# A hybrid decoder layer on one core: kept output weights in buffers of their own, the first value products in a written order, one more dense chunk ahead of GLA's first levels

## Chip, cores, metric

The kernel runs on one core of a Trainium2 chip. The metric is the device time of one execution in microseconds (us); a kernel's time is the median of its runs. The engines are called by the names of the profile: PE is TensorE (PEld its weight loads), DVE is VectorE, ACT is ScalarE, POOL is GpSimd and SP is SyncE, which issues nearly all DMAs. A program keeps instructions of one engine in order; an engine that waits holds up all that stands behind on it.

## What is computed

One layer over 512 tokens of 1024 channels, all in float32. RMSNorm; one input projection `w_in` of 7696 columns, which feeds three branches and their gates: gated linear attention (GLA, 4 heads, chunked, with a low-rank decay), block-sparse softmax attention (MoBA, 8 heads) and a short gated convolution. Each branch is projected to 1024 channels and weighted by a sigmoid gate; the sum goes through an output projection, a norm and a residual add. Then a channel mixer: norm, up-projection to 2 x 2816, a depthwise convolution of width 3, a SiLU gate, the down-projection, a norm and a residual add.

```python
h = rmsnorm(x, g_mix_pre[l])
(gq, gk, gv, gr, glr, mq, mk, mv, sb, sc, sx, glog) = split_cols(h @ w_in[l], IN_SPLITS)
br_a = gla_mixer(gq, gk, gv, gr, glr, gla_w_lr2[l], gla_b_lr[l], gla_norm[l])
br_b = moba_mixer(mq, mk, mv)
br_c = sb * causal_dwconv(sc * sx, sc_conv_w[l])
merged = (gates[..., 0, :] * (br_a @ w_br_gla[l]) + gates[..., 1, :] * (br_b @ w_br_moba[l])
          + gates[..., 2, :] * (br_c @ w_br_sc[l])).astype(x.dtype)
x = x + rmsnorm(merged @ w_out[l], g_mix_post[l])
h = rmsnorm(x, g_ffn_pre[l])
u = causal_dwconv(h @ ffn_w_up[l], ffn_conv_w[l]) + ffn_conv_b[l]
y = (jax.nn.silu(u[..., :D_FF]) * u[..., D_FF:]) @ ffn_w_down[l]
x = x + rmsnorm(y, g_ffn_post[l])
```

## The kernel before

**Products in three parts.** Each float32 operand is split into a high part (`whi`, `hh`, ...: a copy by ScalarE to a shorter format) and a low part (`wlo`, `hl`: VectorE subtracts the high part from the operand). `mm3` (L93) issues three matmuls for each product: high x high, high x low, low x high. A weight tile of 128x1024 is loaded into `raw` (2 buffers), split by `split_w` (L84 and L85) into `whi` and `wlo` (5 buffers each), and then read by 24 matmuls or more. The 128x512 accumulators are PSUM tiles, 3 with the tag "main" and 5 with the tag "side".

**Who sets the order.** PE's order is that of the program text (a manual schedule over the whole layer). The order of ScalarE, VectorE and GpSimd is chosen by a scheduler when the kernel is built, but for the start block (`with tc.manual_schedule(...)` for both), where it is the text's as well.

**Start.** PE runs 14 matmuls on zeros (`warm`, L203), then two matmuls with a row of ones (L207) that spread the gain `grow` over 128 partitions; VectorE copies the two results into `g1` (L208). For each of 4 token tiles of 128: ScalarE squares x and sums (L161), VectorE and GpSimd make the reciprocal root of the mean (L138, L140), VectorE multiplies x by it and by g1 into h (L163), PE transposes h in 8 matmuls (L171), ScalarE and VectorE split the result into `hh` and `hl` (L175, L176). Then the value products: 24 matmuls with 272 columns (256 value columns and the 16 low-rank columns, unit u = 0) and 24 with the other 256 (u = 1). In each half of 4 contraction tiles the three parts alternate. VectorE copies the sums to `v` and `lrt` (L254, L256). The weights of both units come by `load_v` as two pieces of 512 KB each on SP's queue, the 16 columns on ScalarE's queue (L187), and are split at L239 and L244. The transposes of the next tile stand between the two units. The value products end where the transposes of the convolution weights (L326) begin.

**Dense columns and GLA.** The rest of `w_in` is a stream of chunks of 12 matmuls of 128x512 (`cols_cm`, `mm3c`). `main.beside(gen)` interleaves it with a side generator: for each number n that the generator yields, n chunks of the stream go to PE. For each of two channel tiles `ct`, `gla_pair` issues the products across chunks (L486), copies them to `ac` (L489), yields 1, and goes on to the first group of levels: `decayed` makes the operands E (VectorE L509 and L515, ScalarE L510 and L511, GpSimd L514), PE multiplies them (L529 to L532) into PSUM tiles that must be free of the products across.

**Output projection and first up-projection products.** `row_major` keeps 8 accumulators (4 token tiles x 2 halves of 512 columns) and adds contraction tiles 0 to 3 to all of them. Tiles 4 to 7 (`resident` = 4) are split too and kept, and are then added for one token tile after the other, so that each tile's epilogue runs beside the next one's products. `first_up`, called in between, loads and splits the four weight tiles of the first up-projection unit in the same 5 buffers. The epilogue `epi1` squares the sums (L784), makes the statistic (L791, L793), writes x (L796), squares and normalises x into h (L161, L163), and at the last tile issues the first 256 columns of the up-projection (`up_mm`) with the transposes of tiles 2 and 3 between them.

Of the kernel before, what the change touches and what calls it, by code (L numbers as in the profile page):

```python
# [8 lines left out]
F32 = mybir.dt.float32  # L9
# [6 lines left out]
P = 128  # L16
# [15 lines left out]
def hybrid_layer(ctx: ExitStack, tc: tile.TileContext, x, g_mix_pre, w_in, gla_w_lr2, gla_b_lr,  # L32
# [45 lines left out]
    def split_w(src, a, b, sub=None, urgent=True):  # L78
        with tc.high_priority() if urgent else nullcontext():
            hi = wp.tile([P, 1088], F32R, tag="whi", name=nm("whi"), bufs=5)  # L80
            lo = wp.tile([P, 1088], F32R, tag="wlo", name=nm("wlo"), bufs=5)
            hv = hi[:, :a * b].rearrange("p (a b) -> p a b", a=a)
            lv = lo[:, :a * b].rearrange("p (a b) -> p a b", a=a)
            nc.scalar.activation(hv, src, AF.Copy)  # L84
            (sub or nc.vector).tensor_tensor(lv, src, hv.bitcast(F32), op=OP.subtract)  # L85
        return hv, lv

# [67 lines left out]

    st = pool("start", bufs=2, side="right")

    def normed(xt, g, pl):
        ss = sp.tile([P, 1], F32, tag="ss", name=nm("ss"))
        h = pl.tile([P, D], F32, tag="h", name=nm("h"))  # L160
        nc.scalar.activation(h, xt, AF.Square, accum_out=ss)  # L161
        r = rstd(ss, 1, 1.0 / D)
        nc.vector.scalar_tensor_tensor(h, xt, r, g, op0=OP.mult, op1=OP.mult)  # L163
        return h

    def transposed_split(h, th, tl, t, ps_):
        for b in range(2):
# [7 lines left out]
            nc.scalar.activation(hv, pv, AF.Copy)  # L175
            nc.vector.tensor_tensor(lv, pv, hv.bitcast(F32), OP.subtract)  # L176

    def load_v(u):
        raw = rw.tile([P, 2176], F32, tag="raw", name=nm("vraw"))
        n = 272 if u == 0 else 256  # L180
        rv = raw[:, :8 * n].rearrange("p (k c) -> p k c", k=KD)
        c = C_GV + 256 * u
        for k in (0, 4):
            nc.sync.dma_start(rv[:, k:k + 4, :256],
                              w_in[k * P:(k + 4) * P, c:c + 256].rearrange("(k p) c -> p k c", p=P))
            if u == 0 and k == 0:
                nc.scalar.dma_start(rv[:, :, 256:], w_in[:, C_LR:C_LR + 16].rearrange("(k p) c -> p k c", p=P))  # L187
            yield
        yield rv
# [11 lines left out]
    ps = psum()  # L201
    for _ in range(14):
        nc.tensor.matmul(ps, warm[:, :P], warm, start=True, stop=True)  # L203

    for n in range(2):
        ps = psum()
        nc.tensor.matmul(ps, ones, grow[:, n * 512:(n + 1) * 512], start=True, stop=True)  # L207
        nc.vector.tensor_copy(g1[:, n * 512:(n + 1) * 512], ps)  # L208
# [5 lines left out]
    vraw = [list(load_v(0))[-1]]  # L214
    load_x(1)
    vraw.append(list(load_v(1))[-1])
# [18 lines left out]
    def hi_v(u, half):  # L235
        n = 272 if u == 0 else 256
# [9 lines left out]
    def v_mm(ps, t, u, half):  # L246
        n = 272 if u == 0 else 256
        ts_ = slice(t * P, (t + 1) * P)
        hi, lo = wv[u, half]
        mm3(ps[:, :n], [(hh[:, 4 * half + k, ts_], hl[:, 4 * half + k, ts_], hi[:, k], lo[:, k]) for k in range(4)],  # L250
            start=half == 0, stop=half == 1)
# [223 lines left out]
    def gla_pair(ct, across):  # L475
# [14 lines left out]
        yield 1  # L490
# [246 lines left out]
    h2l = h2p.tile([P, KD, T], F32R, name="h2l")  # L737
    ep = pool("epi", bufs=3, side="right")
# [7 lines left out]
    def row_major(w, kk, resident, getl, epilogue, middle=None):  # L746
# [170 lines left out]
```

## Time and profile before

| what | us |
|---|---|
| median of 3 runs | 898.33 (896.80 to 899.42) |
| the profiled execution | 898.33 |
| its span, from the first to the last instruction | 896.5 |
| busy in the span: PE / DVE / ACT / POOL | 880.6 / 454.1 / 337.6 / 75.0 |

A profile line of a timeline gives the start, the time taken, the engine, the line of the kernel, the operation, what it writes and reads, and how often it stands there in a row (x8); behind it, in brackets, how long the engine had been idle and what ended that. A line of the waits gives an engine and line, what it waited for, the total, the number of times and the longest. A window is a stretch of the span with the busy time of an engine in it and the TensorE clock that was granted, 1.00 being full.

### The profile page before, as it was taken

To read this page: it belongs to the slowest core of one execution; us is meant where nothing else is said; L and a number is where in the kernel's file an instruction comes from. 1 tells how busy PE (TensorE), PEld (TensorE's weight loads), DVE (VectorE), ACT (ScalarE), POOL (GpSimd) and SP (SyncE) were. 2 spreads that over 40 slices of the span, in tenths; PEclk is the share of its full clock that TensorE was granted. 3 is DMA by queue.
4 is the path that set the end of the run, shared out by engine and by line. 5 is a ranking of instruction groups with operands and counts; after the bars stand their busy time and mean duration, and the time that the engine had idled before them with its cause. 6 is when DMAs were issued, how large, how long until landed. Compare 5 with 4: busy or idle time off the path is not lost.

```text
span 896.5 us, 11496 instructions
## 1 busy us (share of the span) xinstructions
PE 880.6 (98%) x4723; PEld 728.7 (81%) x4723; DVE 454.1 (51%) x715; ACT 337.6 (38%) x511; POOL 75.0 (8%) x87
## 2 busy tenths in 40 slices
PE   8999999999999999999999989999999999999997
PEld 5988788987777888888888889888888888888885
DVE  5723766487763242423424486655555555533324
ACT  5236654244543223232322355433333333322222
POOL 1000421131100020101101010000000000000000
PEclk8999999999999999999999999999999999999999
DMA  8241231131211324133265123223333322222202
GB/s 264 69 145 51 91 93 51 48 95 49 93 48 48 117 71 131 58 117 94 72 229 169 48 94 95 94 95 98 104 105 107 103 96 94 94 94 94 94 0 94
DMA packets 68616, 85.33 MB, mean 95 GB/s; under 512 B 2693, under 2 KB 62291, under 8 KB 68564
## 3 DMA queue, kind: packets, MB, share of 16 engines
q1 hardware_dynamic: 67522, 84.53, 29.7%
q8 instruction: 37, 0.61, 0.3%
q10 hardware_dynamic: 1042, 0.07, 0.1%
q14 instruction: 15, 0.12, 0.0%
HBM read 82.50 MB, written 2.10 MB: 94 GB/s over the span
## 4 chain that ended last, share of the span: by engine, by line
PE 93%; ACT 3%; DVE 2%; DMA 1%; issue 1%; POOL 0%; ACTq 0%; DVEq 0%; POOLq 0%
PE ps L93 86%; PE ps L633 1%; PE ps L675 1%; PE ps L565 1%; PE ps L658 1%; DMA vraw<-in_w_in_dram 1%; PE ps L531 1%; DMA raw<-in_ffn_w_up_dram 1%; PE ps L171 1%; ACT whi L84 0%; DVE wlo L85 0%; DVE h L163 0%; ACT L432 0%; ACT whi L239 0%; ACT E L510 0%
## 5 line engine op out<-in xcount | busy, mean ns | idle before, releaser
L85 DVE TENSOR_TENSOR wlo<-raw,whi 128x1024 fp32r<-128x1024 f32 x142 | 178.3, 1257 | 235.2 <-ACT whi L84 235.1
L84 ACT ACTIVATE whi<-raw 128x1024 fp32r<-128x1024 f32 x142 | 149.8, 1057 | 253.8 <-PE ps L93 241.1
L93 PE MATMUL ps<-hh,whi 128*128 128x512 f32 x416 | 165.8, 398 | 0.0
L93 PE MATMUL ps<-hh,wlo 128*128 128x512 f32 x416 | 162.2, 390 | 0.0
L93 PE MATMUL ps<-hl,whi 128*128 128x512 f32 x416 | 162.1, 390 | 0.0
L93 PE MATMUL ps<-h2h,whi 128*128 128x512 f32 (+1 forms) x384 | 143.4, 374 | 0.0
L93 PE MATMUL ps<-h2h,wlo 128*128 128x512 f32 (+1 forms) x384 | 143.3, 373 | 0.0
L93 PE MATMUL ps<-h2l,whi 128*128 128x512 f32 (+1 forms) x384 | 143.2, 373 | 0.0
L93 PEld LDWEIGHTS ps<-hh,whi 128*128 128x128 f32 x416 | 78.1, 188 | 19.4 <-issue 3.2
L93 PEld LDWEIGHTS ps<-hh,wlo 128*128 128x128 f32 x416 | 78.1, 188 | 16.8
L93 PEld LDWEIGHTS ps<-hl,whi 128*128 128x128 f32 x416 | 78.2, 188 | 15.3
L93 PEld LDWEIGHTS ps<-h2h,wlo 128*128 128x128 f32 x384 | 73.0, 190 | 12.6
L93 PEld LDWEIGHTS ps<-h2l,whi 128*128 128x128 f32 x384 | 73.0, 190 | 12.5
L93 PEld LDWEIGHTS ps<-h2h,whi 128*128 128x128 f32 x384 | 73.1, 190 | 12.4
L93 PE MATMUL ps<-whi,ahi 128*128 128x512 f32 x176 | 68.5, 389 | 0.0
L93 PE MATMUL ps<-wlo,ahi 128*128 128x512 f32 x176 | 68.5, 389 | 0.0
L93 PE MATMUL ps<-whi,alo 128*128 128x512 f32 x176 | 68.5, 389 | 0.0
L879 DVE TENSOR_TENSOR alo<-a,ahi 128x512 fp32r<-128x512 f32 x22 | 15.2, 692 | 55.9 <-ACT ahi L878 55.9
L878 ACT ACTIVATE ahi<-a 128x512 fp32r<-128x512 f32 x22 | 13.9, 632 | 75.4 <-PE ps L93 65.4
L724 POOL TENSOR_TENSOR gate<-gate 128x512 f32<-128x512 f32 x16 | 24.0, 1502 | 216.7 <-DVE gate L722 200.1
L93 PE MATMUL ps<-whi,hh 128*128 128x256 f32 (+1 forms) x128 | 38.4, 300 | 0.9 <-ACT hh L175 0.9
L93 PEld LDWEIGHTS ps<-wlo,ahi 128*128 128x128 f32 x176 | 33.0, 188 | 6.9
(196 smaller groups left out, 1181.5 us busy)
## 6 DMA issues: line engine op xcount, KB each, us to landing
raw<-in_w_in_dram SPq DMA_DIRECT2D x28, 1024.0 KB, 5.5
raw<-in_ffn_w_up_dram SPq DMA_DIRECT2D x22, 1024.0 KB, 5.1
raw<-in_ffn_w_down_dram SPq DMA_DIRECT2D x11, 1024.0 KB, 4.9
x<-in_x_dram SPq DMA_DIRECT2D x8, 512.0 KB, 7.2
raw<-in_w_out_dram SPq DMA_DIRECT2D x4, 1024.0 KB
vraw<-in_w_in_dram SPq DMA_DIRECT2D x4, 512.0 KB, 6.5
raw<-in_w_br_gla_dram SPq DMA_DIRECT2D x4, 512.0 KB, 3.6
raw<-in_w_br_moba_dram SPq DMA_DIRECT2D x4, 512.0 KB, 3.4
```

Of the source, the lines that this page charges most:

```text
L84: nc.scalar.activation(hv, src, AF.Copy)
L85: (sub or nc.vector).tensor_tensor(lv, src, hv.bitcast(F32), op=OP.subtract)
L93: last = nc.tensor.matmul(ps, l, r, start=start and i == 0 and j == 0, stop=stop and i == n - 1 and j == 2)
L171: nc.tensor.transpose(ps[:, i * P:(i + 1) * P], h[:, k * P:(k + 1) * P], ident)
L531: nc.tensor.matmul(pv[0:64, t], kl[hs, lo], qr[hs, lo], start=True, stop=True)
L565: nc.tensor.matmul(po[:, c], l, v[:, j, cv], start=j == 0, stop=j == i)
L633: nc.tensor.matmul(out_[i, e][:, :n], mq[hs, pair, i * P:(i + 1) * P], mk[hs, pair, :n], start=True, stop=True)
L658: nc.tensor.transpose(ps[:, (i - j) * P:(i - j + 1) * P], pr[i][:, j * P:(j + 1) * P], ident)
L675: nc.tensor.matmul(po[64 * e:64 * e + 64, j * P:], mv[:, j, hd * 64:(hd + 1) * 64], pts[e][j], start=j == 0, stop=j == NT - 1)
L724: nc.gpsimd.tensor_tensor(g, g, acc, op=OP.add)
L878: nc.scalar.activation(hi, a[:, k], AF.Copy)
L879: nc.vector.tensor_tensor(lo, a[:, k], hi.bitcast(F32), OP.subtract)
```

## The change

Three places change; the sums computed are the same.

1. **Start.** 8 warm-up matmuls, the two gain broadcasts, 7 warm-ups, the transposes, 1 warm-up. ScalarE copies the gain to `g1` in halves, VectorE's first multiply is in halves. The 16 low-rank columns move from the first unit to the second, and with them their DMA on ScalarE's queue; the first unit is now the upper 256 value columns. `v_mm` issues all 8 high x high, then 8 low x high, then 8 high x low products; the next tile's transposes come before the last 8 of the second unit. ScalarE copies the sums to `v`. The first split of the dense column weights is pinned behind the last copy to `hh`.
2. **GLA.** `yield 2 - ct`: for ct = 0, two chunks of the stream instead of one stand between the products across and the first levels; the stream's last stretch, behind MoBA, has 96 matmuls instead of 108.
3. **Output projection.** `keep_out` gives the kept tiles 4 and 5 homes in `ahi`/`alo` (four halves of 128x512, buffers that the down-projection uses later) and tiles 6 and 7 in a new pool `khi`/`klo`. The five whi/wlo buffers are then free for the up-projection's splits.

```diff
-    def split_w(src, a, b, sub=None, urgent=True):
...
+    def split_w(src, a, b, home=None):
+        with tc.high_priority():
+            if home is None:
+                home = [wp.tile([P, 1088], F32R, tag=tag, name=nm(tag), bufs=5) for tag in ("whi", "wlo")]
+            hv, lv = [z[:, :a * b].rearrange("p (a b) -> p a b", a=a) for z in home]
+            ins = nc.scalar.activation(hv, src, AF.Copy)
+            if first_splits:
+                after(ins, first_splits.pop(), "the start's own copies come first")
+            nc.vector.tensor_tensor(lv, src, hv.bitcast(F32), op=OP.subtract)
         return hv, lv
...
     def load_v(u):
-        n = 272 if u == 0 else 256
+        n = 272 if u else 256
-        c = C_GV + 256 * u
+        c = C_GV + 256 * (1 - u)
+        if u:
+            nc.scalar.dma_start(rv[:, :, 256:], w_in[:, C_LR:C_LR + 16].rearrange("(k p) c -> p k c", p=P))
...
-    for _ in range(14):
-        nc.tensor.matmul(ps, warm[:, :P], warm, start=True, stop=True)
...
+    warm_up(8)
+    gps = [psum() for _ in range(2)]
     for n in range(2):
-        nc.tensor.matmul(ps, ones, grow[:, n * 512:(n + 1) * 512], start=True, stop=True)
-        nc.vector.tensor_copy(g1[:, n * 512:(n + 1) * 512], ps)
+        nc.tensor.matmul(gps[n], ones, grow[:, n * 512:(n + 1) * 512], start=True, stop=True)
+    warm_up(7)
...
+    def v_mm(ps, t, u, before_lo=None):
+        for j, (l, part) in enumerate(((hh, 0), (hl, 0), (hh, 1))):
+            if j == 2 and before_lo:
+                before_lo()
+            for k in range(KD):
+                nc.tensor.matmul(ps[:, :n], l[:, k, ts_], wv[u, k // 4][part][:, k % 4],
+                                 start=j == 0 and k == 0, stop=j == 2 and k == KD - 1)
...
     def v_out(ps, t, u):
-        nc.vector.tensor_copy(v[:, t, u * 256:(u + 1) * 256], ps[:, :256])
-        if u == 0:
+        nc.scalar.activation(v[:, t, (1 - u) * 256:(2 - u) * 256], ps[:, :256], AF.Copy)
+        if u:
             nc.vector.tensor_copy(lrt[:, t, :16], ps[:, 256:272])
...
     with tc.manual_schedule(engines={nc.scalar.engine, nc.vector.engine}):
-        hn = normed(xts[0], g1, st)
+        ss, hn = squares(xt, st)
+        halves = [slice(n * 512, (n + 1) * 512) for n in range(2)]
+        for n in range(2):
+            nc.scalar.activation(g1[:, halves[n]], gps[n], AF.Copy)
         hi_v(0, 0)
-        lo_v(0, 0)
+        r = rstd(ss, 1, 1.0 / D)
+        for n in range(2):
+            nc.vector.scalar_tensor_tensor(hn[:, halves[n]], xt[:, halves[n]], r, g1[:, halves[n]],
+                                           op0=OP.mult, op1=OP.mult)
+        transposed_split(hn, hh, hl, 0, psum, (lambda: lo_v(0, 0), None))
+        warm_up(1)
         hi_v(0, 1)
-        transposed_split(hn, hh, hl, 0, psum)
         lo_v(0, 1)
         for t in range(NT):
             pa, pb = psum("main"), psum("main")
+            v_mm(pa, t, 0)
             if t < 3:
                 hn = normed(xts[t + 1], g1, st)
             if t == 0:
                 for half in range(2):
                     hi_v(1, half)
                     lo_v(1, half)
-            for half in range(2):
-                v_mm(pa, t, 0, half)
-            if t < 3:
-                transposed_split(hn, hh, hl, t + 1, psum)
             v_out(pa, t, 0)
-            for half in range(2):
-                v_mm(pb, t, 1, half)
+            v_mm(pb, t, 1, (lambda: transposed_split(hn, hh, hl, t + 1, psum)) if t < 3 else None)
             v_out(pb, t, 1)
+            if t == 2:
+                first_splits.append(last_hi[0])
...
-        yield 1
+        yield 2 - ct
...
+    kp = pool("kept", bufs=2, side="right")
...
-                wts.append([z[:, 0] for z in split_w(raw[:, e:e + 1], 1, D)])
+                if keep and kt >= kk - resident:
+                    wts.append(keep(kt, raw[:, e:e + 1]))
+                else:
+                    hl_ = split_w(raw[:, e:e + 1], 1, D)
+                    wts.append([[z[:, 0, n * 512:(n + 1) * 512] for n in range(2)] for z in hl_])
...
+    def keep_out(kt, src):
+        if kt >= 6:
+            home = [kp.tile([P, D], F32R, tag=tag, name=nm(tag)) for tag in ("khi", "klo")]
+            return [[z[:, 0, n * 512:(n + 1) * 512] for n in range(2)] for z in split_w(src, 1, D, home)]
+        halves = []
+        for n in range(2):
+            home = [ah.tile([P, T], F32R, tag=tag, name=nm(tag)) for tag in ("ahi", "alo")]
+            halves.append([z[:, 0] for z in split_w(src[:, :, n * 512:(n + 1) * 512], 1, 512, home)])
+        return [[halves[n][z] for n in range(2)] for z in range(2)]
...
-    row_major(w_out, KD, 4, lambda k: (mh[:, k], ml[:, k]), epi1, first_up)
+    row_major(w_out, KD, 4, lambda k: (mh[:, k], ml[:, k]), epi1, first_up, keep_out)
```

The order of PE at the start, before, from the last of the 14 warm-ups to the first value products (`ps_170` is the accumulator of unit 0, `h_141` tile 0's h):

```order
L203 LDWEIGHTS warm
L203 MATMUL ps_96<-warm 128x512
L207 MATMUL ps_111<-grow,ones 128x512
L207 MATMUL ps_114<-grow,ones 128x512
L171 MATMUL ps_155<-ident,h_141 128x128 x4
L171 MATMUL ps_162<-ident,h_141 128x128 x4
L93 MATMUL ps_170<-whi_148,hh 128x272
L93 MATMUL ps_170<-wlo_149,hh 128x272
L93 MATMUL ps_170<-whi_148,hl 128x272
L93 MATMUL ps_170<-whi_148,hh 128x272
```

and changed, from the last of the 7 warm-ups behind the broadcasts (`ps_173` is unit 0's accumulator, `whi_144`/`whi_169` the two halves of its weights):

```order
L214 LDWEIGHTS warm
L214 MATMUL ps_96<-warm 128x512
L179 MATMUL ps_153<-ident,h_140 128x128 x4
L179 MATMUL ps_161<-ident,h_140 128x128 x4
L214 LDWEIGHTS warm
L214 MATMUL ps_96<-warm 128x512
L267 MATMUL ps_173<-whi_144,hh 128x256 x4
L267 MATMUL ps_173<-whi_169,hh 128x256 x4
L267 MATMUL ps_173<-whi_144,hl 128x256 x4
L267 MATMUL ps_173<-whi_169,hl 128x256 x4
L267 MATMUL ps_173<-wlo_145,hh 128x256 x4
L267 MATMUL ps_173<-wlo_170,hh 128x256 x4
```

A warm-up now stands behind the transposes, and the three parts of the products follow each other in runs instead of alternating.

ScalarE at the start, before, from tile 0's square to the first weight split of unit 1 (L239 are the splits of value weights, L175 the copies to `hh`):

```order
L161 ACTIVATE h_141,ss_140<-x_90 128x1024
L239 ACTIVATE whi_148<-vraw_118 128x1088
L239 ACTIVATE whi_152<-vraw_118 128x1088
L175 ACTIVATE hh<-ps_155 128x4x128
L175 ACTIVATE hh<-ps_162 128x4x128
L161 ACTIVATE h_173,ss_172<-x_91 128x1024
L239 ACTIVATE whi_180<-vraw_123 128x1024
```

and changed (L281 is the copy to g1, L252 the split, L183 the copy to `hh`, L271 the copy to v):

```order
L165 ACTIVATE h_140,ss_139<-x_90 128x1024
L281 ACTIVATE g_89<-ps_105 128x512
L281 ACTIVATE g_89<-ps_106 128x512
L252 ACTIVATE whi_144<-vraw_117 128x1024
L183 ACTIVATE hh<-ps_153 128x4x128
L183 ACTIVATE hh<-ps_161 128x4x128
L252 ACTIVATE whi_169<-vraw_117 128x1024
L165 ACTIVATE h_200,ss_199<-x_91 128x1024
L252 ACTIVATE whi_207<-vraw_121 128x1088
L252 ACTIVATE whi_211<-vraw_121 128x1088
L271 ACTIVATE v<-ps_173 128x256
```

The g1 copies come ahead of the first split, the second split behind the copies to `hh`, and copies to v stand on this engine.

ScalarE around the output projection's epilogue, before, from the first square of tile 3 (`sq_4451`, L784) to its square of x (`h_4465`, L161); L84 are splits of up-projection weights:

```order
L784 ACTIVATE sq_4451,ss_736_4449<-ps_4098 128x512
L175 ACTIVATE h2h<-ps_4423 128x4x128
L161 ACTIVATE h_4404,ss_4403<-x_4072 128x1024
L175 ACTIVATE h2h<-ps_4430 128x4x128
L84 ACTIVATE whi_4242<-raw_4236 128x1024
L84 ACTIVATE whi_4248<-raw_4246 128x1024
L84 ACTIVATE whi_4252<-raw_4246 128x1024
L784 ACTIVATE sq_4455,ss_736_4449<-ps_4099 128x512
L175 ACTIVATE h2h<-ps_4497 128x4x128
L175 ACTIVATE h2h<-ps_4504 128x4x128
L84 ACTIVATE whi_4732<-raw_4730 128x1024
L161 ACTIVATE h_4465,ss_4464<-x_4072 128x1024
```

Ahead of these rows stand `whi_4238` and the squares of tiles 0 to 2. Changed, from the last kept tile to tile 0's second square:

```order
L83 ACTIVATE khi_4242<-raw_4240 128x1024
L83 ACTIVATE ahi_4236<-raw_4222 128x512
L83 ACTIVATE khi_4246<-raw_4240 128x1024
L83 ACTIVATE whi_4252<-raw_4250 128x1024
L83 ACTIVATE whi_4256<-raw_4250 128x1024
L83 ACTIVATE whi_4262<-raw_4260 128x1024
L83 ACTIVATE whi_4266<-raw_4260 128x1024
L83 ACTIVATE whi_4747<-raw_4745 128x1024
L813 ACTIVATE sq_4296,ss_706_4294<-ps_4098 128x512
L813 ACTIVATE sq_4300,ss_706_4294<-ps_4099 128x512
```

All four splits of the first up-projection unit (`whi_4252` to `whi_4266`) and the first of the second unit (`whi_4747`) now stand ahead of tile 0's first square (`sq_4296`).

## Rows read from the trace of the kernel before

**Rows 1.** The page, part 1: busy us (share of the span) and instructions by engine.
```profile
PE 880.6 (98%) x4723; PEld 728.7 (81%) x4723; DVE 454.1 (51%) x715; ACT 337.6 (38%) x511; POOL 75.0 (8%) x87
```

**Rows 2.** Waits of PE: line, releaser, us in total, times, longest us.
```profile
PE ps L171 <- DVE h L163: 5.3, 3, 2.5
...
PE ps L93 <- ACT hh L175: 0.9, 1, 0.9
```

**Rows 3.** Timeline, GLA's first levels: start, us, engine, line, [idle before <-releaser].
```profile
101.25 0.27 PE L531 MATMUL ps<-E 64*64 64x64 f32 x1 [2.02 <-ACT ac L489]
...
99.13 1.17 ACT L510 ACTIVATE E<-E 128x512 f32<-128x512 f32 x2 [2.51 <-DVE E L509]
...
100.73 0.85 ACT L489 ACTIVATE ac<-ps 128x384 f32<-128x384 f32 x2
```

**Rows 4.** Timeline of PE at the start.
```profile
1.40 4.77 PE L203 MATMUL ps<-warm 128*128 128x512 bf16 x14 [1.40 <-DVE warm L200]
6.10 1.98 PE L207 MATMUL ps<-grow,ones 1*128 1x512 f32 x4
10.26 1.09 PE L171 MATMUL ps<-ident,h 128*128 128x128 f32 x8 [2.17 <-DVE h L163]
...
42.33 0.53 PE L326 MATMUL ps<-ident,rows 64*128 64x64 f32 x5
```

**Rows 5.** Windows of PE: stretch, us, busy (instructions), granted clock, DMA share, GB/s.
```profile
1.40:4.60 3.20, 3.20 (x8) 1.00 0.84 262
12.20:18.10 5.90, 5.89 (x25) 0.50 0.70 227
36.33:42.33 6.00, 6.00 (x50) 1.00 0.13 21
95.50:98.44 2.94, 2.94 (x14) 1.00 0.00 0
101.30:110.00 8.70, 8.70 (x122) 1.00 0.42 122
537.10:540.50 3.40, 3.40 (x19) 0.50 0.02 5
```

**Rows 6.** Timelines of SP, ScalarE (ACT) and VectorE (DVE) at the start.
```profile
1.23 0.97 SPq L184 DMA_DIRECT2D vraw<-in_w_in_dram  x2
...
4.55 1.06 ACT L161 ACTIVATE h<-x 128x1024 f32<-128x1024 f32 x1 [1.46 <-DMA x<-in_x_dram]
...
9.55 2.12 ACT L239 ACTIVATE whi<-vraw 128x1088 fp32r<-128x1088 f32 x2 [3.85 <-DMA vraw<-in_w_in_dram]
11.58 1.06 ACT L175 ACTIVATE hh<-ps 128x512 fp32r<-128x512 f32 x2
...
8.12 0.69 DVE L208 COPY g<-ps 128x512 f32<-128x512 f32 x1 [0.17 <-PE ps L207]
8.92 1.28 DVE L163 SCALAR_TENSOR_TENSOR h<-x,rs,g 128x1024 f32<-128x1024 f32 x1
```

**Rows 7.** DMA view: issues, KB each, median us to landing.
```profile
raw<-in_ffn_w_up_dram SPq DMA_DIRECT2D x22, 1024.0 KB, 5.1
...
vraw<-in_w_in_dram SPq DMA_DIRECT2D x4, 512.0 KB, 6.5
...
vraw<-in_w_in_dram ACTq DMA_DIRECT2D x1, 64.0 KB, 8.2
```

**Rows 8.** Timelines of ScalarE and VectorE around the row-wise products.
```profile
502.69 0.60 ACT L784 ACTIVATE sq<-ps 128x512 f32<-128x512 f32 x1 [1.74 <-PE ps L93]
...
523.01 2.96 ACT L84 ACTIVATE whi<-raw 128x1024 fp32r<-128x1024 f32 x3
...
531.48 1.06 ACT L84 ACTIVATE whi<-raw 128x1024 fp32r<-128x1024 f32 x1 [3.04 <-DMA raw<-in_ffn_w_up_dram]
...
528.37 0.21 DVE L791 TENSOR_SCALAR ms<-ss 128x1 f32<-128x1 f32 x1
...
534.52 1.28 DVE L163 SCALAR_TENSOR_TENSOR h<-x,rs,g 128x1024 f32<-128x1024 f32 x1 [0.66 <-POOL rs L140]
```

More of the change, by code (lines that the diff above doesn't have):

```diff
@@ L76, in load_w @@
         return v
-    def split_w(src, a, b, sub=None, urgent=True):
[L79 to L85, printed above, removed]
+    def split_w(src, a, b, home=None):
[7 more added lines that the diff above has]
+            nc.vector.tensor_tensor(lv, src, hv.bitcast(F32), op=OP.subtract)
         return hv, lv
+    first_splits = []
     def mm3(ps, terms, start=True, stop=True):
@@ L153, in hybrid_layer, with squares @@
     hl = hp.tile([P, KD, T], F32R, name="hl")
+    last_hi = [None]
     st = pool("start", bufs=2, side="right")
-    def normed(xt, g, pl):
+    def squares(xt, pl):
         ss = sp.tile([P, 1], F32, tag="ss", name=nm("ss"))
@@ L161, in normed @@
         nc.scalar.activation(h, xt, AF.Square, accum_out=ss)
+        return ss, h
+    def normed(xt, g, pl):
+        ss, h = squares(xt, pl)
         r = rstd(ss, 1, 1.0 / D)
@@ L164, in normed, with transposed_split @@
         return h
-    def transposed_split(h, th, tl, t, ps_):
+    def transposed_split(h, th, tl, t, ps_, between=(None, None)):
         for b in range(2):
@@ L174, in transposed_split @@
             lv = tl[:, 4 * b:4 * b + 4, t * P:(t + 1) * P]
-            nc.scalar.activation(hv, pv, AF.Copy)
+            last_hi[0] = nc.scalar.activation(hv, pv, AF.Copy)
+            if between[b]:
+                between[b]()
             nc.vector.tensor_tensor(lv, pv, hv.bitcast(F32), OP.subtract)
@@ L185, in load_v @@
                               w_in[k * P:(k + 4) * P, c:c + 256].rearrange("(k p) c -> p k c", p=P))
[L186 to L189, printed above, removed]
+        return rv
     grow = st.tile([1, D], F32, name="grow", bufs=1)
@@ L200, in hybrid_layer, with warm_up @@
     nc.vector.memset(warm, 0.0)
-    ps = psum()
-    for _ in range(14):
-        nc.tensor.matmul(ps, warm[:, :P], warm, start=True, stop=True)
+    wps = psum()
+    def warm_up(n):
+        for _ in range(n):
+            nc.tensor.matmul(wps, warm[:, :P], warm, start=True, stop=True)
+    warm_up(8)
+    gps = [psum() for _ in range(2)]
     for n in range(2):
-        ps = psum()
-        nc.tensor.matmul(ps, ones, grow[:, n * 512:(n + 1) * 512], start=True, stop=True)
-        nc.vector.tensor_copy(g1[:, n * 512:(n + 1) * 512], ps)
+        nc.tensor.matmul(gps[n], ones, grow[:, n * 512:(n + 1) * 512], start=True, stop=True)
+    warm_up(7)
     def load_x(t):
@@ L213, in hybrid_layer @@
     load_x(0)
[L214 removed]
+    vraw = [load_v(0)]
     load_x(1)
[L216 removed]
+    vraw.append(load_v(1))
     load_x(2)
@@ L744, in hybrid_layer, with row_major @@
         nc.sync.dma_start(x1[:, t], x[t * P:(t + 1) * P])
-    def row_major(w, kk, resident, getl, epilogue, middle=None):
+    def row_major(w, kk, resident, getl, epilogue, middle=None, keep=None):
         flip[0] = 0
@@ L760, in row_major @@
                         for n in range(2):
-                            mm3(accs[t][n], [(lh[:, ts_], ll[:, ts_], wts[kt][0][:, n * 512:(n + 1) * 512],
-                                                     wts[kt][1][:, n * 512:(n + 1) * 512])], start=kt == 0, stop=False)
+                            mm3(accs[t][n], [(lh[:, ts_], ll[:, ts_], wts[kt][0][n], wts[kt][1][n])],
+                                start=kt == 0, stop=False)
         if middle:
@@ L771, in row_major @@
                     epilogue(t - 1, accs, True)
-                ns = slice(n * 512, (n + 1) * 512)
-                last = mm3(accs[t][n], [(ls[kt][0][:, ts_], ls[kt][1][:, ts_], wts[kt][0][:, ns], wts[kt][1][:, ns])
+                last = mm3(accs[t][n], [(ls[kt][0][:, ts_], ls[kt][1][:, ts_], wts[kt][0][n], wts[kt][1][n])
                                         for kt in range(kk - resident, kk)], start=False)[1]
```

10 lines of the change are left out of this document (4 added, 6 removed).

## The prediction

> **What bounds the kernel now.** I read the page first: PE, TensorE's matmuls, is busy for 880.6 us, 98% of the span [rows 1], so no other engine can be the bound, and a change can help in two ways only: by ending idle time of PE, or by letting it work at full clock. All further views are read for these two. The waits of PE [rows 2] are three for a normalised tile h, 5.3 us in all with the longest 2.5, and one of 0.9 for `hh`; with one of 2.02 for the copies `ac` [rows 3] and the 1.40 us before the first warm-up matmul [rows 4] this is nearly all that PE idles. The windows [rows 5] show the second loss: the clock granted to PE was 0.50 (the 1.2 GHz level) in 12.20 to 18.10 and in 537.10 to 540.50, and 1.00 (2.4 GHz) in the others. Both half-rate stretches follow an idle time of over 2 us: 2.17 before the transposes of 10.26 [rows 4] with 0.9 more for `hh`, and the longest wait for h, 2.5 [rows 2]. The 2.02 us before the matmul of 101.25 [rows 3] left the clock at 1.00 [rows 5].
>
> **The start.** Before, PE runs 14 warm-up matmuls from 1.40, two gain broadcasts (`grow`) from 6.10, and starves from 8.1 to 10.26 [rows 4], since h comes late: VectorE copies the second half of g1 from PSUM at 8.12 and only then multiplies, from 8.92 for 1.28 [rows 6]. ScalarE sat 3.85 us until 9.55 [rows 6] for the value weights, whose last piece is the 64 KB of 16 columns on ScalarE's own queue, 8.2 us from issue to landing; SP's 512 KB pieces take 6.5 [rows 7].
>
> The changed kernel puts the broadcasts behind 8 warm-ups. The first 8 take 3.20 us [rows 5], so the broadcasts start at 4.6 instead of 6.10 and end, 1.98 later [rows 4], at 6.6; seven more warm-ups at the rate of the other six, (4.77 − 3.20) / 6 = 0.26, keep PE busy to 8.4. ScalarE's square of 4.55 [rows 6] ends near 5.7 with the read of its sum (an estimate). It then copies g1 in halves, at 0.53 each (half of the pair at 11.58 [rows 6]): the first at 5.9, the second, behind the second broadcast, at 6.8 to 7.4. VectorE's half multiplies, 0.65 each, follow them, h is ready near 8.1, and the transposes start at 8.4 without idle time. They hold PE to 9.3 (their row says 1.09 [rows 4]; some 0.2 of it lies under the next matmul). The 16-column piece now belongs to the second unit, so the first weight split waits for SP's piece only, 1.2 + 6.5 = 7.7 [rows 6, 7], and ends at 8.8. ScalarE then works in order: two `hh` copies to 9.9, the second weight split to 11.0, the square of tile 1 to 12.2, unit 1's two splits to 13.3 and 14.3. PE's first four products start at 9.4, and from 9.9 it waits 1.1 for the second split; unit 1's second half costs another 0.3. A token tile has 48 products at 6.00 / 48 = 0.125 [rows 5] and 0.85 for the next transposes: 9.4 + 1.4 + 6.0 + 0.85 = 17.65 for tile 0, then 6.85, 6.85 and 6.0: the value products end at 37.35, where they ended at 42.33 [rows 4]. **Start: −5.0**, with bounds of −2.5 (half clock again, or ScalarE late throughout) and −6.4 (none of the waits).
>
> Two warm-ups more cost nothing, since they lie where PE idled. Eight v copies move to ScalarE, at most 0.53 each: per tile it then has 2 × 0.53 + 1.06 (`hh`) + 1.2 (square) = 3.3 us of work in 6.85. The chain to the next h (v copy 0.5, square 1.2, statistic and rstd 0.8, multiply 1.28) is 3.8 against some 4.9 that PE needs up to its next transposes; it is the next to be late, with 1 us in hand. The first column-weight split is pinned behind the last `hh` copy, at about 29, still 8 us before its product.
>
> **GLA's first levels.** PE waits 2.02 us until 101.25 for ScalarE's `ac` copies, begun at 100.73 behind two exponent passes, which had waited 2.51 for VectorE [rows 3]. None of these hangs on the dense chunk. It takes 2.94 us [rows 5]; with 12 more such products ahead PE gets to this point later than the copies, and the whole wait is filled with work that is taken from the end of the stream (96 dense products behind MoBA instead of 108). **First levels: −2.0**, bounds 0 (the copies move back with PE) and −2.0: there is no more to fill. Later steps of GLA come one chunk earlier against the dense columns; their operands hang on the same chain, which PE does not pace, and no other wait there is over the 0.9 of [rows 2].
>
> **Kept output weights.** Four of the five whi/wlo buffers hold kept weights until the row-wise products end, so three of the four splits of the first up-projection weights run only at 523.01, 2.96 us on ScalarE, and VectorE's part of them stands ahead of tile 3's statistic, at 528.37 [rows 8]. Only then can the next load be issued: ScalarE waits 3.04 for it until 531.48, with the square of tile 3 queued behind. h is multiplied from 534.52 to 535.8 [rows 8], 2.5 us too late [rows 2]: PE needed it at 533.3.
>
> With buffers of their own for the kept weights, all four splits and the next unit's first come before the square of tile 0. Tile 3's first square, which stood behind the three splits until 526.0, can then go at about 524.1 (between 523.0, where the splits began, and 526.0) and the statistic at 524.9. Even with the whole old distance from statistic to multiply, 534.52 − 528.37 = 6.15, h is ready at 524.9 + 6.15 + 1.28 = 532.3; without the split that stood between, 1.06, at 531.3. So 1 to 2 us are in hand, the idle 2.4 goes, and the half clock behind it: 3.40 us at 0.50 hold 16 products [rows 5], which at 0.125 take 2.0: 1.4 more. **Epilogue: −3.8**, bounds −1.0 (1.4 us late after all, clock as before) and −4.0. The kept halves add two instructions on ScalarE and two on VectorE, engines busy 38% and 51% [rows 1]. SP's load of g_ffn_post goes behind another weight load; it is read after the down-projection only.
>
> The two clock terms, 2.4 of the start (24 products at half rate, 0.1 each) and 1.4 here, rest on rows: 0.50 behind idle times of 2.2 and 2.5, 1.00 behind 2.02, and at the start no single wait over 1.1 is left. The Trainium skill (TensorE: Matmul & The Clock Gate, section HAM oscillation — how this bites in real kernels) lets the clock fall only behind idle gaps longer than any here; by it neither stretch would come from its gap, and the sum would lack 3.8. The trace speaks against it: 0.50 stands right behind the gap of 2.5 us.
>
> **Sum.** −5.0 − 2.0 − 3.8 = −10.8 on the profiled execution's 898.33 us (span 896.5), which is also the median of the runs shown: **887.5 us**.
>
> **Rivals.**
> 1. The clock does not hold at the start: the waits of 1.1 and 0.3 us come just after it was raised. For it: before, 0.9 us stood among what preceded the fall. Against: 1.4 in all is less than the 2.02 that left it at 1.00. 24 products at half rate: 887.5 + 2.4 = 889.9. Chance 0.13.
> 2. ScalarE paces the value products, with v copies, `hh` copies and squares in order on one queue, and half of the start's gain is lost: 890.0. For it: only 1 us in hand, by estimates. Against: 3.3 of 6.85 us busy. Chance 0.09.
> 3. The extra chunk does not do what it says: the exponent passes ahead of `ac` wait for VectorE, and if VectorE in turn stands behind copies of dense columns, `ac` moves back by the same 2.94. Against: the order of ScalarE and VectorE there is the same but for names. 887.5 + 2.0 = 889.5. Chance 0.05.
> 4. The half-rate stretches do not come from the idle times and both stay: 887.5 + 2.4 + 1.4 = 891.3. Against: the rows above. This is what the page of the Trainium skill named above would make of it. Chance 0.03.
> 5. Slower: ScalarE now meets the first split of the second up-projection unit before tile 0's square (502.69 [rows 8]), and all squares queue behind its load. The load goes out at about 494, an estimate from the splits that free its buffer, and lands 5.1 later [rows 7], at 499. It costs time from a landing after 504 and outweighs 10.8 us only from about 515, 21 us after its issue; the longest landing shown is 8.2 [rows 7]. At 517 it would be 900. Chance 0.02.
>
> **How the numbers follow.** The forecast has 0.68, for 885.5 to 889. The range of **884.5 to 892** adds rivals 1 to 4, and two of the first three together (892); on the other side it takes in waits of the start that don't come. A measurement of this kernel can tell about 0.3%, 2.7 us, from no change, so faster means under 895.6. Every case but the last is below that; of the rivals' chance 0.03 stands for several at once, within 2.7 us of before: faster 0.95, same 0.03, slower 0.02.
>
> **What would show it.** Right: transposes from 8.2 to 8.6 without a wait; the first product near 9.4, one wait of about 1 us behind it; 1.00 in all windows after 5 us; dense columns from 37 to 38; no wait for `ac` over 0.5; none for h at tile 3, and 1.00 there. Wrong: 0.50 in a window before 20 us (rival 1); a wait for `hh` or h in every token tile (2); the 2 us wait at the first levels, only later (3); 0.50 near 530 without idle time (4); ScalarE waiting for a load ahead of tile 0's square (5).

## The result, and the profile after

| | median of runs, us | lowest to highest | profiled span |
|---|---|---|---|
| before | 898.37 (6 runs) | 896.58 to 899.42 | 896.5 |
| changed | 888.50 (6 runs) | 886.19 to 890.47 | 888.7 |

The ratio is 0.9893, 95% interval 0.9868 to 0.9918: 9.9 us less by the medians, where 10.8 had been forecast. But the six times are not spread over their range. Three are 886.2 to 886.6 and three 890.4 to 890.5; none lies near the median, which is only the middle of two outcomes 4 us apart, and the nearest to the forecast's 887.5 is 0.9 from it. All are below the 895.6 that the forecast asked for to call it faster.

PE is busy for 99% of the profiled span, against 98% in [rows 1]. The page's part 1 of the changed kernel:

```profile
PE 880.0 (99%) x4725; PEld 726.4 (82%) x4725; DVE 448.6 (50%) x708; ACT 341.2 (38%) x523; POOL 76.1 (9%) x87
```

and all its waits of PE. Those of [rows 2] and the one of [rows 3] are gone; one for a weight split, foreseen as 1.1, stands in their place:

```profile
PE ps L214 <- DVE warm L209: 1.4, 1, 1.4
PE ps L267 <- ACT whi L252: 0.9, 1, 0.9
```

**Start.** The timeline of PE in this execution, which is one of the 890.4 kind; it answers to [rows 4]:

```profile
1.40 3.60 PE L214 MATMUL ps<-warm 128*128 128x512 bf16 x8 [1.40 <-DVE warm L209]
4.93 3.78 PE L220 MATMUL ps<-grow,ones 1*128 1x512 f32 x4
8.64 3.17 PE L214 MATMUL ps<-warm 128*128 128x512 bf16 x7
11.60 1.88 PE L179 MATMUL ps<-ident,h 128*128 128x128 f32 x8
...
13.35 0.82 PE L267 MATMUL ps<-whi,hh 128*128 128x256 f32 x4
15.11 0.74 PE L267 MATMUL ps<-whi,hh 128*128 128x256 f32 x4 [0.94 <-ACT whi L252]
```

There is no idle time up to the first product, as foreseen, and still the product comes at 13.35 and not at 9.4. Every instruction on the way is slow: the broadcasts took 3.78 us where [rows 4] had 1.98, the seven warm-ups 3.17 (one every 0.42) where 0.26 had been assumed. These are the durations of the lower clock: a 128x512 warm-up every 0.42 us is half the rate of the 0.22 that e1 shows below. The window over the seven warm-ups says otherwise:

```profile
8.64:11.60 2.96, 2.96 (x9) 1.00 1.10 355
...
520.20:545.00 24.80, 24.80 (x210) 1.00 0.20 64
```

The column of the granted clock stands at 1.00 over warm-ups that run at half speed. At the start of this execution the matmul's own duration tells the clock, the column does not. So the sign that the forecast set for rival 1, a 0.50 in a window before 20 us, could not have shown a clock that had not risen.

**First levels.** ScalarE's rows that answer to [rows 3]:

```profile
97.92 1.18 ACT L533 ACTIVATE E<-E 128x512 f32<-128x512 f32 x2 [2.51 <-DVE E L532]
...
99.53 0.85 ACT L512 ACTIVATE ac<-ps 128x384 f32<-128x384 f32 x2
```

The passes and the copies do what they did, VectorE's 2.51 us included, but PE now reaches this place at 99.95, when `ac` is being written, and doesn't wait.

**Epilogue.** The first split of the second unit, the squares of tiles 0 and 3 on ScalarE, and VectorE's statistic and multiply for tile 3, answering to [rows 8]:

```profile
496.56 1.06 ACT L83 ACTIVATE whi<-raw 128x1024 fp32r<-128x1024 f32 x1 [3.12 <-DMA raw<-in_ffn_w_up_dram]
499.10 0.60 ACT L813 ACTIVATE sq<-ps 128x512 f32<-128x512 f32 x1 [1.48 <-PE ps L96]
...
520.38 0.60 ACT L813 ACTIVATE sq<-ps 128x512 f32<-128x512 f32 x1 [0.95 <-PE ps L96]
...
521.26 0.21 DVE L820 TENSOR_SCALAR ms<-ss 128x1 f32<-128x1 f32 x1
...
526.39 1.27 DVE L171 SCALAR_TENSOR_TENSOR h<-x,rs,g 128x1024 f32<-128x1024 f32 x1
```

Then PE's transposes of tile 3, with no wait ahead of them:

```profile
529.62 1.03 PE L179 MATMUL ps<-ident,h 128*128 128x128 f32 x8
```

The statistic comes behind the square at once, h is ready at 527.7 and PE takes it at 529.62: 2.0 us in hand, where 1 to 2 had been forecast. The load of rival 5 came at 496.5. The sign set for that rival is there, ScalarE waiting 3.12 us for the load ahead of tile 0's square, but the wait costs nothing: the split ends at 497.62, and the square stands idle for another 1.48 until PE's sums are complete. The window 520.20 to 545.00 above has the full clock throughout.

### The profile page after: what moved, and what is told of

Its sections match the earlier page's. It is cut to its first block, busy times and chain, and to the rows that moved or that the text cites. A ratio compares the mean times of both kernels' runs of the same rounds, so it can differ in the third digit from the quotient of the medians.

```text
span 888.7 us, 11500 instructions
## 1 busy us (share of the span) xinstructions
PE 880.0 (99%) x4725; PEld 726.4 (82%) x4725; DVE 448.6 (50%) x708; ACT 341.2 (38%) x523; POOL 76.1 (9%) x87
## 4 chain that ended last, share of the span: by engine, by line
PE 99%; ACT 0%; DVE 0%; issue 0%; DVEq 0%; POOLq 0%; ACTq 0%
PE ps L96 88%; PE ps L267 3%; PE ps L656 1%; PE ps L698 1%; PE ps L588 1%; PE ps L681 1%; PE ps L179 1%; PE ps L214 1%; PE ps L554 1%; PE ps L220 0%; PE ps L509 0%; PE ps L555 0%; PE ps L465 0%; PE ps L452 0%; PE ps L607 0%; PE ps L552 0%
## 5 line engine op out<-in xcount | busy, mean ns | idle before, releaser
L86 DVE TENSOR_TENSOR wlo<-raw,whi 128x1024 fp32r<-128x1024 f32 x138 | 173.5, 1258 | 225.2 <-ACT whi L83 225.1
L83 ACT ACTIVATE whi<-raw 128x1024 fp32r<-128x1024 f32 x138 | 145.4, 1056 | 245.9 <-PE ps L96 230.7
L96 PEld LDWEIGHTS ps<-h2l,whi 128*128 128x128 f32 x384 | 72.3, 188 | 12.5
L96 PEld LDWEIGHTS ps<-whi,ahi 128*128 128x128 f32 x176 | 33.0, 188 | 6.9
L96 PEld LDWEIGHTS ps<-whi,alo 128*128 128x128 f32 x176 | 33.0, 188 | 6.9
```

The lines of the kernel that those rows point to most:

```text
L83: ins = nc.scalar.activation(hv, src, AF.Copy)
L86: nc.vector.tensor_tensor(lv, src, hv.bitcast(F32), op=OP.subtract)
L96: last = nc.tensor.matmul(ps, l, r, start=start and i == 0 and j == 0, stop=stop and i == n - 1 and j == 2)
```

## Where the time went, stretch by stretch

Four points of PE's timeline cut an execution: the end of the value products, the first up-projection product, tile 3's transposes, the end of the span. In us, from the profiled executions (e1 is the changed kernel again, e3 and e4 have one part of the change alone):

| stretch | before | changed | e1 | e3 chunk only | e4 kept only |
|---|---|---|---|---|---|
| up to the end of the value products | 42.33 | 41.12 | 36.88 | 41.73 | 41.60 |
| to the first up-projection product | 481.52 | 479.00 | 479.00 | 479.19 | 482.87 |
| to tile 3's transposes | 12.10 | 9.50 | 9.50 | 11.96 | 9.50 |
| to the end | 360.55 | 359.08 | 359.02 | 359.02 | 359.03 |
| span | 896.5 | 888.7 | 884.4 | 891.9 | 893.0 |

## Experiments

**e1: the changed kernel again.** No edit.

> The changed kernel itself once more. Its six times stand in two groups, 886.2 to 886.6 and 890.4 to 890.5, and its profiled execution (span 888.7) is of the second. Theory A (the clock at the start decides): again two groups 4 us apart; if the profile is of the lower group, the two gain broadcasts take 2.0 us instead of 3.78, the seven warm-ups behind them 1.5 instead of 3.2, the transposes start at 8.2 to 8.6 instead of 11.60, and from the dense columns on both executions run alike. Rival B (the 4 us come from another place, such as a landing of a load): in a profile of the lower group the broadcasts still take 3.8 and the difference stands elsewhere.

Four times: 886.13, 886.32, 886.51 and 890.26. The profiled execution (span 884.4) is of the lower kind:

```profile
1.40 3.25 PE L214 MATMUL ps<-warm 128*128 128x512 bf16 x8 [1.40 <-DVE warm L209]
4.58 1.98 PE L220 MATMUL ps<-grow,ones 1*128 1x512 f32 x4
6.49 1.69 PE L214 MATMUL ps<-warm 128*128 128x512 bf16 x7
8.02 1.04 PE L179 MATMUL ps<-ident,h 128*128 128x128 f32 x8
...
9.30 0.74 PE L267 MATMUL ps<-whi,hh 128*128 128x256 f32 x4
10.73 0.74 PE L267 MATMUL ps<-whi,hh 128*128 128x256 f32 x4 [0.69 <-ACT whi L252]
```

The broadcasts take 1.98, the transposes start at 8.02, the first product at 9.30: the forecast's start, nearly to the tenth (8.4 and 9.4). From the second stretch on, the table's columns for the two executions agree within 0.06. So the 4 us stand wholly in the start, and they go with the time at which PE's clock rises: in e1 it was up when the broadcasts started, in the other execution it was not, and the matmuls kept the lower rate to the end of the transposes, about 13.3. (e12 below shows a course between the two.)

**e2: the start alone.** `yield 1` as before, kept tiles in the whi/wlo buffers as before.

> Only the first part of the change (start and value products). Theory A: two groups here too, 1.2 us and 5.2 us below the kernel before (898.4): 897.2 and 893.2; waits of 2 us at the first levels and of 2.5 us at token tile 3 as before. Rival (the start gains only together with the other parts, or ScalarE paces the value products): one group, less than 1 us below.

892.86 to 893.05 three times and 897.00 to 897.17 three times, against 898.87 for the kernel before: 5.9 and 1.8 below. Theory A holds here alone, and the old waits stand:

```profile
PE ps L179 <- DVE h L171: 2.4, 1, 2.4
PE ps L554 <- ACT ac L512: 2.0, 1, 2.0
```

**e3: the chunk alone.**

```diff
-        yield 1
+        yield 2 - ct
```

> Only one more dense chunk ahead of GLA's first levels. Theory: the 2.0 us wait for the ac copies goes and nothing takes its place: 2.0 to 2.5 us below before, 896.1. Rival (given back: the copies move back with the chunk, or the stream's last stretch lacks the 12 products as cover): 898.4, with a new wait behind MoBA.

893.98 to 895.99, median 894.01: 4.9 below, twice what was expected. The wait for `ac` is gone from PE's waits; by the table that is 2.3 us in the second stretch, and nothing is given back behind MoBA. The rest is no merit of the chunk. PE still waits 2.31 us for tile 3's h, but this time no half-rate stretch follows:

```profile
533.00:545.00 12.00, 12.00 (x102) 1.00 0.17 50
```

and the last stretch is 1.53 shorter; another 0.6 is in the start, which e3 does not touch. The mean granted clock listed for each execution says that this profile is no exception: 0.995 here and in three more of the five, 0.993 in the slowest (895.99), as if the stretch had come in that one alone. In e2 all six are listed with 0.997 or 0.998, which fits its profile, where the stretch is there:

```profile
535.50:538.80 3.30, 3.30 (x18) 0.50 0.00 0
```

**e4: the kept weights alone.** `split_w` with `home`, `keep_out` and the pool `kept`, the rest as before.

> Only the kept output weights in buffers of their own. Theory: the idle time of 2.45 us at token tile 3 goes and with it the stretch of 0.50 granted clock behind it: 3.8 to 4.1 us below before, 894.5, and 1.00 in the window of 3.4 us behind the transposes of tile 3. Rival (the half-rate stretch does not come from the idle time): 2.4 us below, 896.0, and 0.50 still there.

893.57 to 895.77, median 895.49, against 898.87: 3.4 below. The wait for h at tile 3 (2.6 in the table) and the half rate behind it (1.5) are gone, as expected. The waits that are left:

```profile
PE ps L170 <- DVE h L162: 2.9, 2, 2.2
PE ps L530 <- ACT ac L488: 2.0, 1, 2.0
```

The wait for `ac`, 1.99 us, is the same as ever, but here the clock fell behind it; and behind tile 3's transposes it did not:

```profile
101.00:104.90 3.90, 3.90 (x22) 0.58 0.00 0
531.00:545.00 14.00, 14.00 (x120) 1.00 0.17 50
```

This takes back 1.35 us (second stretch, 482.87 against 481.52), which is why the part alone measured less than 4.1.

**e5: 14 warm-ups ahead of the broadcasts.**

```diff
-    warm_up(8)
+    warm_up(14)
...
-    warm_up(7)
+    warm_up(1)
```

> The changed kernel with 14 warm-ups ahead of the two gain broadcasts and 1 between them and the transposes (16 in all, as now). In the profiles with 14 in a row (before and two others) these took 4.8 to 5.3 us and the broadcasts behind them 1.98 each time, at full clock. Theory A (two groups because the clock is up or not when the broadcasts start): one group; the broadcasts start at 6.1 to 6.7 and end at 8.1 to 8.7, the first product comes at 10.6 to 11.2, 1.3 to 1.9 later than in the lower group: 887.7 to 888.4. Rival (the two groups have another cause): still two groups 4 us apart.

887.26 to 888.54, median 888.33: no 4 us step in four executions. The profile is of the lowest; the other three are 888.24 to 888.54, and no profile shows what the 1.0 us between them is.

```profile
1.40 4.88 PE L214 MATMUL ps<-warm 128*128 128x512 bf16 x14 [1.40 <-DVE warm L209]
6.21 1.98 PE L220 MATMUL ps<-grow,ones 1*128 1x512 f32 x4
...
10.31 0.74 PE L267 MATMUL ps<-whi,hh 128*128 128x256 f32 x4
```

**e6: broadcasts that read 128 rows.**

```diff
-    grow = st.tile([1, D], F32, name="grow", bufs=1)
-    nc.scalar.dma_start(grow, g_mix_pre)
-    ones = st.tile([1, P], F32, name="ones", bufs=1)
+    grow = st.tile([P, D], F32, name="grow", bufs=1)
+    nc.gpsimd.memset(grow, 0.0)
+    nc.scalar.dma_start(grow[0:1], g_mix_pre)
+    ones = st.tile([P, P], F32, name="ones", bufs=1)
```

> The changed kernel with the two broadcasts reading 128 rows (the gain in row 0, zeros from GpSimd in the others) instead of one row; 8, 7 and 1 warm-ups as now, the sum unchanged. Theory A1 (PE's clock does not rise while the one-row broadcasts run, and so comes 10 us late when it is not up before them): one group near 886.4, the broadcasts at most 2.9 us. Rival A2 (only the 8 warm-ups ahead count, whatever the broadcasts read): two groups as now, 886.4 and 890.4.

888.23 and 888.50, 889.53 and 889.58: neither theory's times. Not decided: the zeros had to be written ahead of the gain's load, which was then issued at 2.05 instead of 0.79, and PE waited 1.80 us for it. The bound of 2.9 us for the broadcasts failed too; they took 3.42 in the profile, which is of the slower pair.

```profile
1.41 3.59 PE L215 MATMUL ps<-warm 128*128 128x512 bf16 x8 [1.41 <-DVE warm L210]
6.81 3.42 PE L221 MATMUL ps<-grow,ones 128*128 128x512 f32 x4 [1.80 <-DMA grow<-in_g_mix_pre_dram]
10.06 1.68 PE L215 MATMUL ps<-warm 128*128 128x512 bf16 x7
```

The seven warm-ups behind these broadcasts ran at full rate, so the clock rose before they began, while 128 rows were read; but the broadcasts also started 1.9 us later than in the first profile of the changed kernel (6.81 against 4.93). Whether the one-row form or the time keeps it down stays open.

**e7: the gain by a spreading DMA.** `nc.scalar.dma_start(g1, bcast_row(g_mix_pre))`; no broadcasts, no copies of g1.

> The changed kernel with the gain read by one DMA of 512 KB that spreads it over 128 partitions, on ScalarE's queue; no broadcasts on PE and no copies of g1, 16 warm-ups in a row. Theory A: one group, since PE runs warm-ups only until the transposes; clock up by 6 us. The extra 512 KB lie beside x and the value weights, 512 KB each, so these land up to 1.5 us later: 886.5 to 888. Rival (the start is bound by loads): over 888.5.

887.60 to 887.66 in four runs: the two outcomes do not show. The price is the load beside x, which lands at 5.95 instead of 4.4 to 4.7, and PE starves for h before the transposes:

```profile
8.86 1.23 PE L179 MATMUL ps<-ident,h 128*128 128x128 f32 x8 [2.45 <-DVE h L277]
...
10.17 0.74 PE L261 MATMUL ps<-whi,hh 128*128 128x256 f32 x4
...
5.95 1.06 ACT L165 ACTIVATE h<-x 128x1024 f32<-128x1024 f32 x1 [3.43 <-DMA x<-in_x_dram]
```

**e8: value products in the old order.** `mm3` in two halves, transposes between the units.

> The changed kernel with the value products in the old order: the three parts alternate for each contraction tile, in two halves, and the next transposes stand between the units. Two groups remain. Theory (the written order lets PE work on high parts while the low parts are still made): the first products wait for hl and wlo of the first half and then for the second half's, 1.0 to 1.5 us more than now; the rest of the loop as now: groups at 887.6 and 891.6. Rival (the order is worth nothing, only the earlier h counts): groups at 886.4 and 890.4.

889.37 to 889.86 and 893.41 to 893.62: 3.4 and 3.1 above the changed kernel's two outcomes, over twice the price expected. PE's waits:

```profile
PE ps L179 <- DVE h L171: 2.1, 3, 0.9
...
PE ps L96 <- DVE ms L141: 0.7, 1, 0.7
```

**e9: as e7, with the load behind x.** The DMA of g1 on SP's queue after `load_x(0)`, 20 warm-ups.

> As e7 (gain spread by one 512 KB DMA, no broadcasts on PE), but the load goes on SP's queue between x of tile 0 and the first value weights, and 20 warm-ups run ahead of the transposes. In e7 the load shared the way with x, which landed at 5.95 instead of 4.4 to 4.7, and h was late by 2.5 us. Theory A with the loads in order: x lands at 4.4, the gain at 6.0, h is ready at 8.0, the first value weights land at 8.0 as in e7, the first product comes at 9.7 in every execution: one group at 886.6 to 887.2. Rival (the loads share the way whatever their order): h late again, 887.6 as e7.

887.61 to 888.08, median 887.86: the rival's time, but not its reason. The loads did come in order (x at 4.50, the gain at 6.85, the weights at 8.35), and h came earlier than in e7; but ScalarE's copies to `hh` stand behind the split of the last load, PE waits for them, and the first product is hardly earlier (9.94 against 10.17):

```profile
9.94 0.74 PE L261 MATMUL ps<-whi,hh 128*128 128x256 f32 x4 [0.75 <-ACT hh L183]
...
4.50 1.06 ACT L165 ACTIVATE h<-x 128x1024 f32<-128x1024 f32 x1 [2.44 <-DMA x<-in_x_dram]
...
8.35 1.06 ACT L246 ACTIVATE whi<-vraw 128x1024 fp32r<-128x1024 f32 x1 [2.69 <-DMA vraw<-in_w_in_dram]
...
6.85 1.42 DVE L277 SCALAR_TENSOR_TENSOR h<-x,rs,g 128x512 f32<-128x512 f32 x2 [1.01 <-DMA g<-in_g_mix_pre_dram]
```

**e10: 11 warm-ups ahead of the broadcasts, 4 behind.**

> The changed kernel with 11 warm-ups ahead of the broadcasts and 4 behind them. In the profiles with 14 or 15 in a row (4.77 to 5.26 us for 14) the rise came after 8 to 10 of them at the lower rate. Theory A: with 11 the clock is up before the broadcasts in every execution, which start at 5.4 to 6.0: one group, 0.5 below e5: 887.2 to 888. Rival (the rise can come later than 11 warm-ups): a second group 4 us higher.

886.21 to 887.38, median 886.94, ratio to before 0.9867 (0.9854 to 0.9880), a little under the times expected, and in four runs none of the upper kind. The broadcasts start at 5.66 and take 1.98:

```profile
1.40 4.33 PE L214 MATMUL ps<-warm 128*128 128x512 bf16 x11 [1.40 <-DVE warm L209]
5.66 1.98 PE L220 MATMUL ps<-grow,ones 1*128 1x512 f32 x4
...
9.76 0.74 PE L267 MATMUL ps<-whi,hh 128*128 128x256 f32 x4
```

This is the lowest mean of the versions run: 886.87, against 887.98 for the ten executions of the changed kernel, and 0.5 above the lower outcome. The gain is the missing upper kind alone, and four executions are few: if the upper kind came in four of ten here too, four without it would be seen in 13 of 100 cases, eight (with e5's) in 2 of 100.

**e11: the 16 columns back in the first unit.** `n = 256 if u else 272`, the load and the copy to `lrt` with u = 0.

> The changed kernel with the 16 low-rank columns back in the first unit. Their piece landed at 9.5 in the kernel before, and the first weight split waits for it. Two groups. Theory (this piece would be what h then waits behind, since the copies to hh stand behind the split on ScalarE): in the lower group the first split moves from 7.1 to 9.5, hh and the first product by as much, 2.0 to 2.4 us more: 888.6; in the upper group, where the split starts at 9.24 anyway, next to nothing: 890.6. Rival (the piece is hidden): groups as now, 886.4 and 890.4.

888.16 and 889.04, 889.95, 890.21. The lowest is 1.8 above the changed kernel's lower outcome, as expected, 889.95 and 890.21 lie where the upper outcome was, and 889.04 belongs to neither. None of the lower kind was profiled. In the profile, an execution of the upper kind, the first split does start on the landing of that piece, but `hh` is not before 12.69 there anyway:

```profile
9.54 1.11 ACT L252 ACTIVATE whi<-vraw 128x1088 fp32r<-128x1088 f32 x1 [0.21 <-DMA vraw<-in_w_in_dram]
```

**e12: old order of the products, transposes late.** As e8, but the transposes stand in the middle of the second unit.

> The value products in the old alternating order, but the next tile's transposes in the middle of the second unit, 12 products later than in e8 (which cost 3.1 us in both groups, with PE waiting 2.1 us for h in three tiles). Theory (two thirds of e8's price are the place of the transposes, the rest is the order at the first tile): no waits for h, 0.9 to 1.2 us above the changed kernel: groups at 887.5 and 891.5. Rival (the price is the alternating order): 889.5 and 893.5 as e8.

888.15 to 888.50 and 892.16 to 892.31: 2.1 and 1.9 above the changed kernel. So of e8's 3.1 to 3.4, some 2 are the alternating order and 1.2 the place of the transposes; I had it the other way round. The longest wait is for a low part, which VectorE makes behind others (from 14.48 on, in the profiled execution):

```profile
PE ps L96 <- DVE wlo L257: 1.5, 1, 1.5
...
PE ps L96 <- DVE ms L141: 0.4, 1, 0.4
```

Its start shows a third course: eight warm-ups all at the lower rate, and the clock up in the course of the broadcasts.

```profile
1.40 3.59 PE L214 MATMUL ps<-warm 128*128 128x512 bf16 x8 [1.40 <-DVE warm L209]
4.92 2.24 PE L220 MATMUL ps<-grow,ones 1*128 1x512 f32 x4
7.10 1.68 PE L214 MATMUL ps<-warm 128*128 128x512 bf16 x7
```

## Why the forecast came out as it did

**The time was right, the picture at the start was of one outcome only.** 888.5 lies in the range, but the forecast's course of events is that of the lower kind, 886.4, and its sum is 1.1 short of that: each part gained more than its term when the clock was up. Four of the ten executions (those of e1 among them) lose 4.2 at the start, and that the median, with three executions of either kind, falls near the forecast is luck.

**Start, −5.0.** Measured −5.45 in e1 and −1.21 in the other execution; the start of before itself differs by 0.7 between profiles (42.33, and 41.73 and 41.60 in e3 and e4, which do not touch it). The step that failed is "so the broadcasts start at 4.6 instead of 6.10 and end, 1.98 later, at 6.6; seven more warm-ups at the rate of the other six". Both rates were read behind 14 warm-ups in a row, where the clock had risen among them; I carried them over to broadcasts that stand behind eight. The 3.20 for the eight was misread besides: it is the width of the window, and in that trace the eight take 3.48. Eight are too few in four of ten executions: they take 3.25 where the rise comes among them (e1), and 3.6 where it doesn't. What followed from an early h was right: the wait for the second split is 0.69 (forecast 1.1), a tile takes 6.75 (22.29 − 15.54 in e1's transposes; forecast 6.85), ScalarE never paced the loop (rival 2 is out), and the old order would have cost 1.9 to 3.4 of it (e8, e12).

**Rival 1** named the right resource, but the wrong moment. The clock does not fall for the waits of 1.1 and 0.3; where it fails, it has not risen yet. And it costs 4.2 instead of 2.4, since the broadcasts, the warm-ups and the transposes run at half rate, not the first 24 products. That its 889.9 lies near the upper outcome is no support for it.

**First levels, −2.0.** Right: −2.33 alone (e3) and −2.52 with the rest. The bound "there is no more to fill" was short by some tenths: from the first product of the levels to the next dense one it is 3.42 us in e2, with a wait of 2.01, and 1.08 in e3, so that 0.3 is saved beside the wait. Rival 3 is out: ScalarE's copies kept their place.

**Epilogue, −3.8.** Right in its place and sum: 12.10 to 9.50 is 2.60 for the wait, 1.47 to 1.53 for the half rate behind it, 4.1 in all. Rival 5 is out: the load could have come 1.5 us later without moving the square.

**The clock behind idle times.** "0.50 behind idle times of 2.2 and 2.5, 1.00 behind 2.02" was read as an order by length. It is none: e4 shows 0.58 over 3.9 us behind 1.99, e3 1.00 behind 2.31, and e7 runs at full rate behind 2.45. Of ten idle times between 1.99 and 2.45 us in the profiles of before, e2, e3, e4 and e7, six had a half-rate stretch behind them or beginning within them. Such a stretch cost 1.35 to 1.55 where it could be priced (1.35 in e4, 1.47 to 1.53 in before, 1.55 in e2, whose last stretch is 360.57).

At the start the idle time need not be the cause at all. In e4 PE stops at 8.39, at the end of the broadcasts, and the clock is down at 8.70 already, when PE has idled for 0.3 of its 2.17 us:

```profile
8.39:8.60 0.21, 0.00 (x0) 1.00 0.81 282
8.70:10.50 1.80, 0.00 (x0) 0.50 1.08 350
```

The idle time of 2.17 behind two broadcasts went with half rate in all three profiles that have it (before, e3, e4), that of 2.45 in e7, which has no broadcasts, did not. So what PE did ahead of the idle time may count as much as the length; no run separates the two.

That the stretch at tile 3 went away with the wait is shown in the profiles of e4 and of the changed kernel, whose ten executions are all listed with a mean granted clock of 0.998 or 0.999. That it would have come without the change is only likely, as e3 shows. With no idle time over 1 us behind the first warm-up, the changed kernel's profiles have no 0.50 before the last products are through, so rival 4, by which both stretches stay, is out. The rule of the Trainium skill (TensorE: Matmul & The Clock Gate, section HAM oscillation — how this bites in real kernels), by which only gaps longer than any here let the clock fall, does not agree with e4's 0.58 behind 1.99 us.

**The parts do not simply add.** e2, e3 and e4 alone are 5.9 (or 1.8), 4.9 and 3.4 below before; together that would be 14.2 (or 10.1), measured are 12.5 (886.4 in e1 against 898.87) and 8.6 (890.26). The chunk alone had 1.53 of the epilogue's clock, which can't be gained twice. By the profiles the parts do add once the clock and the start are set right: without the 1.53 and the 0.60 of the start, e3's span is 2.47 below before; without the 0.73 of the start and with the 1.35 given back, e4's is 4.12 below; e2's start, which ends at 41.07, is 1.26 shorter. Together that is 7.85; the changed kernel's profile, of the same kind at the start as e2's, is 7.8 below before.

## What to carry to other kernels

Count what runs before the clock is up at its lower rate: a rate read behind a long warm-up doesn't hold for work that is moved ahead into it, and three more warm-ups ahead of the moved work (e10) were worth more on the mean than starting it early. When a kernel's times stand in two groups, profile both before reading a median; here one showed a gain of 1.2 us at a place that yields 5.5 in the other. An idle time of PE of 2 us should be priced with the chance (six of ten here) of some 1.5 us of half rate beside it, and a part that is measured alone carries that chance with it.

## What was not expected of the hardware

- The granted clock of the windows read 1.00 over the first stretch of an execution in which a 128x512 matmul came every 0.42 us instead of every 0.22 (3.17 us for seven, against 1.69 in e1).
- After broadcasts that started with the clock not up, PE stayed at the lower rate for 8 us (the first profile of the changed kernel, 4.93 to about 13.3), although it did not idle there; in e12 the clock rose during the broadcasts. What decides is not settled: e6 was meant to show it and did not.
- The clock fell within an idle time, 0.3 us after PE had stopped (e4, between 8.60 and 8.70), and not only behind it.
- The same wait of 2.0 us at the same place was followed by half rate in one profile (e4) and not in two others (before, e2).
